# Delta-rule triangular systems of a diffusion block: layout change through DRAM instead of VectorE transposes, forward systems solved in transposed form

## The chip, the cores and the metric

The kernel runs on one core of a Trainium2 chip. The metric is device time in microseconds (us) of one execution on that core, the median of several runs. A profile of one execution goes with it: its instructions per engine (PE, the matmul engine; DVE, VectorE; ACT, ScalarE; POOL, GpSimd; SP, which issues most DMAs), their waits, and the granted clock of the matmul engine.

## The reference

One block over 512 latent tokens with 256 context tokens, width 1024, all in fp32: three token mixers in parallel (a chunked gated DeltaNet with 8 heads in both directions, a Hyena long convolution, an RG-LRU), each projected and merged by gates computed from the input, then a gated convolutional FFN. The change lies in the DeltaNet. Per head, direction and 64-token chunk it needs the inverse of a unit triangular 64x64 matrix:

```
m = jnp.where(strict, jnp.einsum('bhnid,bhnjd->bhnij', kb, k) * decay, 0.0)
eye = jnp.eye(cs, dtype=m.dtype)
t_inv = lax.linalg.triangular_solve(eye + m, ..., left_side=True, lower=True)
u = jnp.einsum('bhnij,bhnjd->bhnid', t_inv, v * beta[..., None])
w = jnp.einsum('bhnij,bhnjd->bhnid', t_inv, kb * jnp.exp(gc)[..., None])
```

A scan over the 12 chunks follows, forward and backward, and uses `t_inv` in each step.

## The kernel before, in words

**Weights and projections.** Every projection takes a weight tile of 128x1024 in fp32. `load_w` (L164) loads it by a DMA on SP's queue (L168) into one of three raw buffers; `split` makes a high part (L155 on ACT, L157 on POOL) and a low part, raw minus high (L160, on POOL or DVE), each in a ring of two; PE then runs three matmuls per product (L173 to L175, `mm3`). A raw buffer is free for the next DMA once its low part has been made, so SP's L168 waits for L160. A gate tile (24 projections of 512 columns, evicted by ACT at L594, stored by SP at L595) and a value tile (24 of 512 and 24 of 256 columns, evicted by ACT L502 and DVE L505 to L507, then ACT L903, six PE transposes L911, ACT L912, store L913) alternate in the part around the change. Names in this text: v0 to v7 are the value tiles, g0 to g11 the gate tiles.

**The systems.** `gram` (L803) multiplies keys by keys on PE and masks the products on DVE into three SBUF tiles: `M1[0]` and `M1[1]` hold the chunks that each direction needs first, `M3` the rest of both. Each 64x64 matrix is split in two 32x32 diagonal blocks and an off-diagonal one. `solve` (L831) handles one tile: it brings its 128 diagonal blocks into a layout of one block per partition, by 4 DVE transposes of 32 partitions x 1024 (L839), sets X to the identity on POOL (L841, L842), runs 31 elimination steps of a multiplication (L847) and a subtraction (L849) on DVE, brings the inverses back by 4 transposes (L857) and makes a transposed copy of two quarters by 2 more (L859, `Wu`). The off-diagonal blocks follow: per eighth, 16 matmuls for z (L873), a copy on ACT (L874), 16 matmuls for r (L877), a copy on ACT (L878). The finished matrices go to the DRAM tile `wad` by SP (L886, L893), from which the scan steps load them.

**What sets the order.** A scheduler orders the instructions of every engine when the kernel is built, and each engine and each DMA queue works through its list strictly in order. `run` (L931) offers it the pieces: `solve_first(0)` and `solve_first(1)` with v0, g0 to v5, g5, then `solve_second` (tile `M3`) with v6, g6, v7, g7 and g8 to g11. After that come the 12 scan steps (`step`, L996; their matmuls at L1025, L1035, L1043), which alternate with half gate tiles and with pieces of the modulation (L1068 to L1074). The first instruction that needs the second solve's result on PE is the z block L873 of `M3`, and the first one behind its r blocks in the changed kernel is the scan's L1043.

Of the kernel before, what the change touches and what calls it, by code (L numbers as in the profile page):

```python
# [10 lines left out]
F32 = mybir.dt.float32  # L11
F32R = mybir.dt.float32r
AF = mybir.ActivationFunctionType
ALU = mybir.AluOpType
# [3 lines left out]
P = 128  # L18
# [43 lines left out]
def seq(off, kb, n):  # L62
    return [off + kb * i for i in range(n)]
# [10 lines left out]
def tile_block(ctx: ExitStack, tc: tile.TileContext, I: dict, out: bass.AP, dbg=None, upto=99):  # L74
    nc = tc.nc
    sb = ctx.enter_context(tc.tile_pool(name="sb", bufs=1))
    pp = ctx.enter_context(tc.tile_pool(name="pp", bufs=1, space=PSUM))
    dr = ctx.enter_context(tc.tile_pool(name="dr", bufs=1, space=DRAM))
# [4 lines left out]
    def shaped(ap, shape):  # L83
        shape = list(shape)
        if len(shape) == 2:
            return ap
        names = "abcde"[:len(shape) - 1]
        return ap.rearrange("p (%s) -> p %s" % (" ".join(names), " ".join(names)),
                            **{n: d for n, d in zip(names[1:], shape[2:])})

    def at(off, shape, dt=F32, kb=None):

        n = int(np.prod(shape[1:]))
        size = int(kb * 256) if kb else n
        assert n <= size and off * 256 + size <= ARENA * 256, (shape, off, kb)
        key = (off, size, dt)
        if key not in regions:
            regions[key] = nc.alloc_sbuf_tensor_at(f"region{len(regions)}", [P, size], dt, offset=base + int(off * 1024)).ap()
        return shaped(regions[key][0:shape[0], 0:n], shape)

    def ring(kb, offs):
        return Ring(at, kb, offs)
# [22 lines left out]
    act = nc.scalar.activation  # L125
    stt = nc.vector.scalar_tensor_tensor
    vtt = nc.vector.tensor_tensor
    gtt = nc.gpsimd.tensor_tensor
    mmul = nc.tensor.matmul
    load = nc.sync.dma_start  # L130
# [627 lines left out]
    M1 = [at(84 + 8 * d, [P, 4, NH, 64]) for d in range(2)]  # L758
    M3 = at(100, [P, 2, 2, NH, 64])
    first, second = {0: [0, 1, 2, 3], 1: [0, 1, 4, 5]}, {0: [4, 5], 1: [2, 3]}  # L760
# [39 lines left out]
                act(KQ[h // 4][:, h % 4, :, 0, :], tp.rearrange("p n (c i) -> p (n c) i", i=64), AF.Copy)  # L800


    def gram(i, hf):  # L803
        lat, hs = i >= 2, slice(hf * 4, hf * 4 + 4)
        gp = dn([P, 4, 2, 64] if lat else [P, 4, 64])
        for h in range(4):
            for c in range(2):
                rc = slice(c * 64, c * 64 + 64)
                if lat:
                    kq = KQ[hf][:, h, (i - 2) * 2 + c]  # L810
                    mmul(gp[rc, h], kq[:, 0, :], kq, start=True, stop=True)
                else:
                    kt = KTc[hf][:, h, (i * 2 + c) * 64:(i * 2 + c + 1) * 64]
                    mmul(gp[rc, h, :], kt, kt, start=True, stop=True)
        g_ = gp[:, :, 0, :] if lat else gp
        for d in range(2):
            db = DB[d][i][:, hs, :]
            if i in first[d]:
                vtt(M1[d][:, first[d].index(i), hs, :], g_, db, op=ALU.mult)
            else:  # L820
                for c in range(2):
                    rc = slice(c * 64, c * 64 + 64)
                    vtt(M3[d * 64:d * 64 + 64, second[d].index(i), c, hs, :], g_[rc], db[rc], op=ALU.mult)
            if lat:
                at_ = atr([P, 4, 64])
                vtt(at_, gp[:, :, 1, :], db, op=ALU.mult)
                load(wad[d, i, :, 1, hf * 256:hf * 256 + 256], at_.rearrange("p h i -> p (h i)"))

    vtr = nc.vector.transpose

    def solve(dirs, M, NX_, tmr, eng):  # L831


        N, X = NX_
        tt_ = vtt if eng == "dve" else gtt
        for qd in range(4):
            b, d = qd % 2, dirs[qd // 2]
            rows_ = slice(qd * 32, qd * 32 + 32)
            vtr(N[rows_] if d == 0 else N[rows_].rearrange("p j i -> p i j"),  # L839
                M[rows_, :, b * 32:b * 32 + 32].rearrange("p a i -> p i a"))  # L840
        nc.gpsimd.memset(X, 0.0)  # L841
        nc.gpsimd.memset(X.rearrange("p a b -> p (a b)")[:, ::33], 1.0)  # L842
        yield
        for j in range(31):
            r = 31 - j
            tmp = tmr([P, r, j + 1])
            tt_(tmp, N[:, j + 1:, j].unsqueeze(2).to_broadcast([P, r, j + 1]),  # L847
                X[:, j, 0:j + 1].unsqueeze(1).to_broadcast([P, r, j + 1]), op=ALU.mult)
            tt_(X[:, j + 1:, 0:j + 1], X[:, j + 1:, 0:j + 1], tmp, op=ALU.subtract)  # L849
            yield  # L850

        Wu = N
        for qd in range(4):
            b, d = qd % 2, dirs[qd // 2]
            rows_ = slice(qd * 32, qd * 32 + 32)
            xi = X[rows_] if d == 0 else X[rows_].rearrange("p j i -> p i j")
            vtr(M[rows_, :, b * 32:b * 32 + 32].rearrange("p a i -> p i a"), xi)  # L857
            if b == d:
                vtr(Wu[rows_].rearrange("p a j -> p j a"), xi.rearrange("p i j -> p j i"))  # L859
        yield  # L860

        Z = X.rearrange("p a b -> p (a b)")
        for half in range(2):
            zp = dn([P, 16, 32])
            rp = dn([P, 16, 32])
            for c in range(2):
                d = dirs[c]
                pj = slice(c * 64 + d * 32, c * 64 + d * 32 + 32)
                pi = slice(c * 64 + (1 - d) * 32, c * 64 + (1 - d) * 32 + 32)
                ci = slice((1 - d) * 32, (1 - d) * 32 + 32)  # L870
                for a in range(16):
                    e = half * 16 + a
                    mmul(zp[pi, a, :], M[pj, e, ci], Wu[pj, e, :], start=True, stop=True)  # L873
                act(Z[pi, half * 512:half * 512 + 512], zp[pi].rearrange("p a b -> p (a b)"), AF.Copy)  # L874
                for a in range(16):
                    e = half * 16 + a
                    mmul(rp[pj, a, :], Z[pi, e * 32:e * 32 + 32], M[pi, e, ci], start=True, stop=True)  # L877
                act(M[pj, half * 16:half * 16 + 16, ci], rp[pj], AF.Copy, scale=-1.0)  # L878
            yield

    def solve_first(d):
        yield from solve((d, d), M1[d].rearrange("p t h i -> p (t h) i"),
                         [at(158 + 14 * d + 4 * i, [P, 32, 32]) for i in range(2)], ring(1, seq(166 + 2 * d, 1, 2)),
                         "dve")
        for a, i in enumerate(first[d]):
            load(wad[d, i, :, 0, :], M1[d][:, a].rearrange("p h i -> p (h i)"))  # L886

    def solve_second():
        yield from solve((0, 1), M3.rearrange("p t c h i -> p (t c h) i"),
                         [at(180 + 4 * i, [P, 32, 32]) for i in range(2)], ring(1, seq(188, 1, 2)), "dve")  # L890
        for d in range(2):
            for t, i in enumerate(second[d]):
                load(wad[d, i, :, 0, :].rearrange("(c j) x -> j c x", c=2),  # L893
                     M3[d * 64:d * 64 + 64, t].rearrange("p c h i -> p c (h i)"))
# [21 lines left out]
    for h in range(NH + 2):  # L916
        if h < NH:
            kss_[h] = key(h)
        if h == 0:
            query_out(NH - 1, sqs[NH - 1])  # L920
        if 0 < h <= NH:
            kns_[h - 1] = key_out(h - 1, kss_[h - 1])
        if h > 1:
            key_cols(h - 2, kns_[h - 2])
        if h >= 6:
            for i in [(0, 1), (2,), (3, 4), (5,)][h - 6]:
                gram(i, 0)
    for i in (0, 1, 4, 5, 2, 3):
        gram(i, 1)
# [26 lines left out]
    gates = [lambda f=f: gate(*f, "act", "pool") for f in fill[:NFILL]]  # L956
    work = [w_ for p_ in zip(values, gates) for w_ in p_] + values[len(gates):] + gates[len(values):]
    run([solve_first(0), solve_first(1)], work[:NW1])
    run([solve_second()], work[NW1:])
    for nm, x_ in (("kdd", kdd), ("vd", vd), ("rowd", rowd)):  # L960
        dump(nm, x_)
# [667 lines left out]
```

## Time and profile before

| | us |
|---|---|
| runs | 2179.06, 1700.55, 1703.49 |
| median | 1703.49 |
| the profiled execution: its own time | 1699.04 |
| the profiled execution: span, first to last instruction | 1696.9 |
| mean granted clock of TensorE in it | 0.957 of full |

The first run was disturbed and is far above the other two. The median is a measured time of the whole program; the span leaves out 2.1 us around the first and last instruction. The trace gives times from the start of the span; the part with the systems lies between 560 and 780 us.

### The profile page before, as it was taken

To read this page: it belongs to the slowest core of one execution; us is meant where nothing else is said; L and a number is where in the kernel's file an instruction comes from. 1 tells how busy PE (TensorE), PEld (TensorE's weight loads), DVE (VectorE), ACT (ScalarE), POOL (GpSimd) and SP (SyncE) were. 2 spreads that over 40 slices of the span, in tenths; PEclk is the share of its full clock that TensorE was granted. 3 is DMA by queue.
4 is the path that set the end of the run, shared out by engine and by line. 5 is a ranking of instruction groups with operands and counts; after the bars stand their busy time and mean duration, and the time that the engine had idled before them with its cause. 6 is when DMAs were issued, how large, how long until landed. Compare 5 with 4: busy or idle time off the path is not lost. (4 is left out here: it accounts for less than half of the span.)

```text
span 1696.9 us, 23679 instructions
## 1 busy us (share of the span) xinstructions
PE 1554.4 (92%) x9176; PEld 1264.1 (74%) x9176; DVE 1202.8 (71%) x1756; ACT 618.8 (36%) x1014; POOL 587.0 (35%) x407
## 2 busy tenths in 40 slices
PE   6989989889999988987899999999999999999998
PEld 1657767668787766875687777778878788888876
DVE  4677798765655999553675566777665899989873
ACT  3447878753454222231111150332222433333311
POOL 3752444433535351221333313222321234333441
PEclk7989999989999998788999999999999999999999
DMA  8522222234534332467889646322452123232331
GB/s 304 183 93 69 81 74 70 98 111 136 166 108 135 117 92 90 124 196 190 243 238 247 220 173 229 112 87 86 157 191 89 63 87 99 95 104 93 106 112 50
DMA packets 93057, 225.66 MB, mean 133 GB/s; under 512 B 9963, under 2 KB 30699, under 8 KB 92176
## 3 DMA queue, kind: packets, MB, share of 16 engines
q1 hardware_dynamic: 92112, 217.86, 40.9%
q0 software_dynamic: 832, 6.29, 0.9%
q8 instruction: 72, 1.18, 0.3%
q14 instruction: 41, 0.34, 0.1%
HBM read 190.45 MB, written 33.66 MB: 132 GB/s over the span
## 5 line engine op out<-in xcount | busy, mean ns | idle before, releaser
L173 PE MATMUL bank<-region,region 128*128 128x512 f32 (+1 forms) x2032 | 761.4, 376 | 23.8 <-DVE region L507 7.6
L175 PE MATMUL bank<-region,region 128*128 128x512 f32 (+1 forms) x2032 | 755.4, 373 | 24.6 <-DVE region L160 21.3
L174 PE MATMUL bank<-region,region 128*128 128x512 f32 (+1 forms) x2032 | 756.9, 373 | 5.0 <-DVE region L439 2.9
L173 PEld LDWEIGHTS bank<-region,region 128*128 128x128 f32 x2032 | 389.5, 192 | 101.6 <-ACT region L539 9.0
L175 PEld LDWEIGHTS bank<-region,region 128*128 128x128 f32 x2032 | 389.7, 192 | 97.7 <-DVE region L160 27.8
L174 PEld LDWEIGHTS bank<-region,region 128*128 128x128 f32 x2032 | 390.3, 192 | 69.6 <-DVE region L439 4.9
L160 DVE TENSOR_TENSOR region<-region,region 128x1024 fp32r<-128x1024 f32 (+2 forms) x241 | 269.8, 1133 | 173.0 <-ACT region L155 94.9
L155 ACT ACTIVATE region<-region 128x1024 fp32r<-128x1024 f32 (+2 forms) x209 | 178.4, 865 | 427.4 <-PE bank L174 130.0
L160 POOL TENSOR_TENSOR region<-region,region 128x1024 fp32r<-128x1024 f32 (+1 forms) x64 | 155.3, 2431 | 251.2 <-ACT region L155 210.8
L157 POOL TENSOR_SCALAR region<-region 128x1024 fp32r<-128x1024 f32 (+1 forms) x96 | 113.0, 1178 | 337.8 <-PE bank L174 151.2
L1443 DVE SCALAR_TENSOR_TENSOR region<-bank,pc,region 128x441 f32<-128x441 f32 (+2 forms) x352 | 224.8, 688 | 4.3 <-ACT region L1432 0.7
L505 DVE SCALAR_TENSOR_TENSOR region<-bank,pc,region 128x511 f32<-128x511 f32 (+1 forms) x56 | 34.1, 630 | 51.1 <-ACT region L502 47.3
L1074 DVE SCALAR_TENSOR_TENSOR region<-region,cc,region 128x1024 f32<-128x1024 f32 x28 | 42.1, 1504 | 35.9 <-DMA region<-in_w_mod_dram 35.5
L1012 POOL TENSOR_TENSOR region<-region,region 128x512 f32<-128x512 f32 x32 | 45.8, 1460 | 38.3 <-DMA region<-rowd 37.3
L502 ACT ACTIVATE region<-bank,pc 128x512 f32<-128x512 f32 (+1 forms) x40 | 23.0, 597 | 96.2 <-PE bank L175 96.2
L1455 POOL TENSOR_TENSOR region<-region,region 128x512 f32<-128x512 f32 x22 | 34.3, 1560 | 66.1 <-DVE region L1443 52.2
L1048 DVE SCALAR_TENSOR_TENSOR region<-region,egl,bank 128x128 f32<-128x128 f32 x160 | 42.3, 340 | 19.2 <-PE bank L1043 19.2
L1025 PE MATMUL bank<-region,region 128*64 128x128 f32 x608 | 38.9, 287 | 9.4 <-DVE region L1048 9.3
L1025 PEld LDWEIGHTS bank<-region,region 128*64 128x64 f32 x608 | 35.9, 145 | 14.6 <-DVE region L1048 6.3
L1037 ACT ACTIVATE region<-bank 128x512 f32<-128x512 f32 x24 | 14.3, 598 | 88.1 <-PE bank L1035 87.7
L594 ACT ACTIVATE region<-bank 128x512 f32<-128x512 f32 x32 | 18.8, 587 | 70.1 <-PE bank L175 66.0
L1035 PE MATMUL bank<-region,region 64*64 64x128 f32 x384 | 28.3, 298 | 12.7 <-DVE region L1029 6.9
(286 smaller groups left out, 1697.1 us busy)
## 6 DMA issues: line engine op xcount, KB each, us to landing
region<-in_w_in_dram SPq DMA_DIRECT2D x97, 512.0 KB, 3.6
region<-in_w_mod_dram SPq DMA_DIRECT2D x48, 512.0 KB, 6.7
region<-in_ffn_up_dram SPq DMA_DIRECT2D x44, 512.0 KB, 3.5
region<-in_w_proj_dram SPq DMA_DIRECT2D x24, 512.0 KB, 3.7
region<-in_ffn_down_dram SPq DMA_DIRECT2D x22, 512.0 KB, 3.4
gated<-region SPq DMA_DIRECT2D x32, 256.0 KB, 2.1
region<-gated SPq DMA_DIRECT2D x32, 256.0 KB, 3.5
kdd<-region SPq DMA_DIRECT2D x16, 384.0 KB, 2.8
```

The source lines that it names most:

```text
L155: act(hi, raw, AF.Copy)
L157: nc.gpsimd.tensor_scalar(hi, raw, 1.0, 0.0, op0=ALU.mult, op1=ALU.add)
L160: (vtt if e_lo == "dve" else gtt)(lo, raw, hi.bitcast(F32), op=ALU.subtract)
L173: mmul(ps, lh, rh, start=start, stop=False)
L174: mmul(ps, lh, rl, start=False, stop=False)
L175: mmul(ps, ll, rh, start=False, stop=stop)
L1012: gtt(wq[d][:, hs], KQ[hf][:, :, chs[d] - 4], eg[:, hs].unsqueeze(2).to_broadcast([P, 4, 2, 64]), op=ALU.mult)
L1025: mmul(X[hf][rcs[d], h, :], wq[d][:, hf * 4 + h, kind], S[d][:, hf * 4 + h, :], start=(kind == 0 or h == 0), stop=(kind == 0))
L1048: stt(S[d][:, h], S[d][:, h], egl[:, d, c, i, h:h + 1], p3[hf][d][:, h % 4], op0=ALU.mult, op1=ALU.add)
L1074: stt(acc, w_, cc[:, k, 0:1], acc, op0=ALU.mult, op1=ALU.add)
L1443: stt(uv[:, ro, co], pv_[:, ri, ci], w[:, a * 3 + b:a * 3 + b + 1], uv[:, ro, co], op0=ALU.mult, op1=ALU.add)
L1455: gtt(uu[0], uu[0], uu[1], op=ALU.mult)
```

## The change

Two DRAM tiles are added, `md` for the masked matrices and `xd` for the inverses. `gram` stores each tile of `M1` and `M3` to `md` as soon as its second half is masked (12 stores). `solve` loads its blocks from `md` straight into the one-per-partition layout, by 4 loads of 32x32 pieces of 32 fp32 numbers. Forward systems are needed transposed there: in `solve_first(0)` the elimination runs on the transposed form instead (`upper`: same operations, same sizes, with the index order reversed), and in `solve_second` the forward half is loaded into X and copied transposed into N by ACT. After the elimination ACT makes a transposed copy of X in N (L867), both are stored to `xd` (L868, L869), and 4 loads bring the inverses into M (L872) and 2 the transposed ones into `Wu` (L874). In all 30 DVE transposes go; 48 DMAs (12 + 12 + 6 + 18) on SP's queue and 4 ACT copies come. In the changed kernel z is L888, r L892, their copies L889 and L893, the stores of finished matrices L900 and L907, the elimination L861 and L863, the scan's matmuls L1039, L1049 and L1057, the value transposes L925.

```diff
     def gram(i, hf):
...
             if i in first[d]:
-                vtt(M1[d][:, first[d].index(i), hs, :], g_, db, op=ALU.mult)
+                t = first[d].index(i)
+                vtt(M1[d][:, t, hs, :], g_, db, op=ALU.mult)
+                if hf:
+                    load(md[d, :, t * 8:t * 8 + 8, :], M1[d][:, t])
...
+                if hf:
+                    t = second[d].index(i)
+                    load(md[2, d * 64:d * 64 + 64, t * 16:t * 16 + 16, :], M3[d * 64:d * 64 + 64, t].rearrange("p c h i -> p (c h) i"))
...
-            vtr(N[rows_] if d == 0 else N[rows_].rearrange("p j i -> p i j"),
-                M[rows_, :, b * 32:b * 32 + 32].rearrange("p a i -> p i a"))
+            load((N if upper or d else X)[rows_], md[n, rows_, :, b * 32:b * 32 + 32].rearrange("j a i -> a j i"))
+        if not upper and 0 in dirs:
+            act(N[0:64], X[0:64].rearrange("p j i -> p i j"), AF.Copy)
...
+            if upper:
+                to, row = slice(0, r), slice(r, 32)
+                of = r
+            else:
+                to, row = slice(j + 1, 32), slice(0, j + 1)
+                of = j
...
         Wu = N
...
-            vtr(M[rows_, :, b * 32:b * 32 + 32].rearrange("p a i -> p i a"), xi)
+        act(N, X.rearrange("p j i -> p i j"), AF.Copy)
+        load(xd[n, 0], X)
+        load(xd[n, 1], N)
+        for b, d, rows_ in quads:
+            there = int(not (upper or d))
+            load(M[rows_, :, b * 32:b * 32 + 32], xd[n, there, rows_].rearrange("a j i -> j a i"))
             if b == d:
-                vtr(Wu[rows_].rearrange("p a j -> p j a"), xi.rearrange("p i j -> p j i"))
+                load(Wu[rows_], xd[n, 1 - there, rows_].rearrange("a i j -> i a j"))
```

The scheduler then builds another order. Three places of it follow.

SP, before: what the queue holds where the finished first matrices are stored (L886), with weight loads (L168) between; no load that a solve needs stands there.

```order
L886 DMA wad<-region_2966 128x512 x2
L595 DMA gated<-region_4108 128x512
L168 DMA region_720<-in_w_in_dram 128x1024
L886 DMA wad<-region_2966 128x512 x2
L886 DMA wad<-region_2967 128x512 x2
```

SP, after: the same stores (now L900; region_2966 is `M1[0]`, region_2967 `M1[1]`), with the loads of the second `Wu` quarter (L874) and the last load into the second solve's N (region_4895, L846).

```order
L168 DMA region_902<-in_w_in_dram 128x1024
L874 DMA region_3880<-xd 32x32x32
L872 DMA region_2967<-xd 32x32x32 x2
L874 DMA region_3880<-xd 32x32x32
L927 DMA vd<-region_3099 128x6x128
L900 DMA wad<-region_2966 128x512 x4
L900 DMA wad<-region_2967 128x512 x2
L595 DMA gated<-region_4122 128x512
L846 DMA region_4895<-md 32x32x32
L900 DMA wad<-region_2967 128x512 x2
```

The last input of the second solve has moved behind six stores of finished first matrices and one gate store.

DVE, before: the second solve's start (region_4875 is its N, region_4876 its X), behind the transposes of the first two.

```order
L859 STREAM_TRANSPOSE region_3866<-region_3867 32x32x32
L857 STREAM_TRANSPOSE region_2967<-region_3867 32x32x32 x2
L859 STREAM_TRANSPOSE region_3866<-region_3867 32x32x32
L847 TENSOR_TENSOR region_4883<-region_4875,region_4876 128x31
L849 TENSOR_TENSOR region_4876<-region_4876,region_4883 128x31
```

DVE, after: the second solve's start (region_4895 is its N, region_4896 its X).

```order
L505 SCALAR_TENSOR_TENSOR region_3088<-bank_64,pc,region_3088 128x511
L506 SCALAR_TENSOR_TENSOR region_3088<-bank_64,pc,region_3088 128x511
L507 SCALAR_TENSOR_TENSOR region_3088<-bank_64,pc,region_3088 128x510
L160 TENSOR_TENSOR region_722<-region_902,region_721 128x1024
L861 TENSOR_TENSOR region_4904<-region_4895,region_4896 128x31
L863 TENSOR_TENSOR region_4896<-region_4896,region_4904 128x31
```

The second solve has moved behind the evictions of v7 and one low part of a weight tile, that of the gate tile g12 which the scan's first half gate uses.

PE, before: the second solve's z and r (region_2968 is `M3`), behind g11 and ahead of the scan's L1035.

```order
L175 MATMUL bank_66<-region_80,region_442 128x512
L873 MATMUL bank_67<-region_4875,region_2968 32x32 x16
L873 MATMUL bank_69<-region_4875,region_2968 32x32 x16
...
L873 MATMUL bank_69<-region_4875,region_2968 32x32 x16
L877 MATMUL bank_70<-region_2968,region_4876 32x32 x16
L1035 MATMUL bank_65<-region_5420,region_147 64x128 x8
L1035 MATMUL bank_66<-region_5420,region_147 64x128 x8
```

PE, after: the last z and r blocks of the second first-solve (region_2967), behind the last projection of g10.

```order
L175 MATMUL bank_65<-region_80,region_722 128x512
L888 MATMUL bank_67<-region_2967,region_3881 32x32 x16
...
L892 MATMUL bank_68<-region_2967,region_3881 32x32 x16
L925 MATMUL bank_67<-ident,region_3022 128x128 x2
L925 MATMUL bank_68<-ident,region_3022 128x128 x4
L173 MATMUL bank_66<-region_80,region_441 128x512
```

PE, after: the second solve's z and r (region_4895 is `Wu`), some 48 rows further on.

```order
L1049 MATMUL bank_66<-region_5444,region_147 64x128 x8
L173 MATMUL bank_63<-region_80,region_721 128x512
...
L175 MATMUL bank_63<-region_80,region_722 128x512
L888 MATMUL bank_67<-region_4895,region_2968 32x32 x16
L888 MATMUL bank_69<-region_4895,region_2968 32x32 x16
...
L892 MATMUL bank_70<-region_2968,region_4896 32x32 x16
L1057 MATMUL bank_69<-region_1199,region_5445 128x128
```

Six blocks of z and r of the first systems have come between g10 and g11, g11 has come behind them, and the second solve's blocks stand behind the scan's first L1049 and 12 projections, directly ahead of L1057.

## Rows read from the trace of the kernel before

**Rows 1.** The page, part 1: busy time, share and instructions of PE.
```profile
PE 1554.4 (92%) x9176; PEld 1264.1 (74%) x9176; DVE 1202.8 (71%) x1756; ACT 618.8 (36%) x1014; POOL 587.0 (35%) x407
```

**Rows 2.** Busy by stretch: length, PE, PEld, DVE, ACT, POOL, clock, DMA share, GB/s.
```profile
600.00:620.00 20.00, 15.45 (x68) 12.93 (x69) 20.00 (x56) 5.87 (x9) 13.90 (x2) 0.83 0.24 75
...
680.00:700.00 20.00, 20.00 (x196) 16.83 (x195) 5.02 (x13) 3.53 (x6) 1.42 (x2) 0.50 0.24 80
...
760.00:780.00 20.00, 13.65 (x134) 11.50 (x132) 4.34 (x4) 4.49 (x9) 0.00 (x0) 0.62 0.68 179
```

**Rows 3.** Groups by line, 545 to 800 us: busy, mean ns, idle before, releaser.
```profile
L160 POOL TENSOR_TENSOR region<-region,region 128x1024 fp32r<-128x1024 f32 x18 | 57.8, 3216 | 89.8 <-ACT region L155 89.8
...
L839 DVE STREAM_TRANSPOSE region<-region 32x1024 f32<-32x1024 f32 x12 | 25.4, 2120 | 0.3
L857 DVE STREAM_TRANSPOSE region<-region 32x1024 f32<-32x1024 f32 x12 | 25.3, 2104 | 0.3
...
L155 ACT ACTIVATE region<-region 128x1024 fp32r<-128x1024 f32 x18 | 19.0, 1056 | 19.6 <-PE bank L174 12.4 <-DMA wad<-region 3.2 <-issue 2.5
...
L859 DVE STREAM_TRANSPOSE region<-region 32x1024 f32<-32x1024 f32 x6 | 11.9, 1990 | 0.0
...
L1074 DVE SCALAR_TENSOR_TENSOR region<-region,cc,region 128x1024 f32<-128x1024 f32 x7 | 9.0, 1285 | 21.3 <-DMA region<-in_w_mod_dram 21.2
...
L874 ACT ACTIVATE region<-bank 32x512 f32<-32x512 f32 x12 | 7.1, 588 | 18.5 <-PE bank L873 15.3 <-DVE region L857 3.2
```

**Rows 4.** PE's timeline: start, length, line, shape, count, idle before and releaser.
```profile
571.95 0.82 PE L911 MATMUL bank<-ident,region 128*128 128x128 f32 x6
...
601.26 0.58 PE L173 MATMUL bank<-region,region 128*128 128x256 f32 x1 [4.17 <-DVE region L507]
...
615.16 0.79 PE L175 MATMUL bank<-region,region 128*128 128x512 f32 x1 [3.29 <-POOL region L160]
...
630.11 0.82 PE L911 MATMUL bank<-ident,region 128*128 128x128 f32 x6
...
644.61 0.82 PE L911 MATMUL bank<-ident,region 128*128 128x128 f32 x6
...
650.83 1.91 PE L873 MATMUL bank<-region,region 32*32 32x32 f32 x32 [5.41 <-DVE region L859]
...
660.11 1.19 PE L873 MATMUL bank<-region,region 32*32 32x32 f32 x32 [0.94 <-DVE region L859]
...
777.40 1.83 PE L1043 MATMUL bank<-region,region 64*128 64x128 f32 x28
```

**Rows 5.** DVE's timeline in the second solve: start, length, line, shape, count.
```profile
674.67 0.21 DVE L847 TENSOR_TENSOR region<-region,region 128x31 f32<-128x31 f32 x1
...
685.00 0.42 DVE L847 TENSOR_TENSOR region<-region,region 128x255 f32<-128x255 f32 x1
...
717.60 2.40 DVE L849 TENSOR_TENSOR region<-region,region 128x156 f32<-128x156 f32 x1
...
736.43 2.09 DVE L859 STREAM_TRANSPOSE region<-region 32x1024 f32<-32x1024 f32 x1
```

**Rows 6.** POOL's timeline: start, length, line, shape, count, idle before.
```profile
603.56 13.90 POOL L160 TENSOR_TENSOR region<-region,region 128x1024 fp32r<-128x1024 f32 x2 [9.10 <-ACT region L155]
...
632.04 2.40 POOL L160 TENSOR_TENSOR region<-region,region 128x1024 fp32r<-128x1024 f32 x1 [1.32 <-ACT region L155]
```

**Rows 7.** DMA issues: names, queue, count, KB each, median us to landing.
```profile
gated<-region SPq DMA_DIRECT2D x32, 256.0 KB, 2.1
...
kdd<-region SPq DMA_DIRECT2D x16, 384.0 KB, 2.8
region<-kdd SPq DMA_DIRECT2D x24, 256.0 KB, 7.6
```

**Rows 8.** Line L827 (stores to `wad`), SP's queue: issue time in ns, min/median/max.
```profile
L827 SPq DMA_DIRECT2D wad<-region x16: 319/320/655, 543.0 to 584.0; - x16
```

More of the change, by code (lines that the diff above doesn't have):

```diff
@@ L800, in key_cols @@
                 act(KQ[h // 4][:, h % 4, :, 0, :], tp.rearrange("p n (c i) -> p (n c) i", i=64), AF.Copy)
+    md, xd = dr.tile([3, P, 32, 64], F32, name="md"), dr.tile([3, 2, P, 32, 32], F32, name="xd")
     def gram(i, hf):
@@ L827, in gram, with solve @@
                 load(wad[d, i, :, 1, hf * 256:hf * 256 + 256], at_.rearrange("p h i -> p (h i)"))
-    vtr = nc.vector.transpose
-    def solve(dirs, M, NX_, tmr, eng):
+    def solve(n, dirs, M, NX_, tmr):
         N, X = NX_
[L835 to L838, printed above, removed]
-            vtr(N[rows_] if d == 0 else N[rows_].rearrange("p j i -> p i j"),
-                M[rows_, :, b * 32:b * 32 + 32].rearrange("p a i -> p i a"))
+        upper = dirs == (0, 0)
+        quads = [(qd % 2, dirs[qd // 2], slice(qd * 32, qd * 32 + 32)) for qd in range(4)]
+        for b, d, rows_ in quads:
+            load((N if upper or d else X)[rows_], md[n, rows_, :, b * 32:b * 32 + 32].rearrange("j a i -> a j i"))
+        if not upper and 0 in dirs:
+            act(N[0:64], X[0:64].rearrange("p j i -> p i j"), AF.Copy)
         nc.gpsimd.memset(X, 0.0)
@@ L845, in solve @@
             r = 31 - j
+            if upper:
[4 more added lines that the diff above has]
+                of = j
             tmp = tmr([P, r, j + 1])
-            tt_(tmp, N[:, j + 1:, j].unsqueeze(2).to_broadcast([P, r, j + 1]),
-                X[:, j, 0:j + 1].unsqueeze(1).to_broadcast([P, r, j + 1]), op=ALU.mult)
-            tt_(X[:, j + 1:, 0:j + 1], X[:, j + 1:, 0:j + 1], tmp, op=ALU.subtract)
+            vtt(tmp, N[:, to, of].unsqueeze(2).to_broadcast([P, r, j + 1]),
+                X[:, of, row].unsqueeze(1).to_broadcast([P, r, j + 1]), op=ALU.mult)
+            vtt(X[:, to, row], X[:, to, row], tmp, op=ALU.subtract)
             yield
         Wu = N
[L853 to L856, printed above, removed]
-            vtr(M[rows_, :, b * 32:b * 32 + 32].rearrange("p a i -> p i a"), xi)
+        act(N, X.rearrange("p j i -> p i j"), AF.Copy)
+        load(xd[n, 0], X)
+        load(xd[n, 1], N)
+        for b, d, rows_ in quads:
+            there = int(not (upper or d))
+            load(M[rows_, :, b * 32:b * 32 + 32], xd[n, there, rows_].rearrange("a j i -> j a i"))
             if b == d:
-                vtr(Wu[rows_].rearrange("p a j -> p j a"), xi.rearrange("p i j -> p j i"))
+                load(Wu[rows_], xd[n, 1 - there, rows_].rearrange("a i j -> i a j"))
         yield
@@ L881, in solve_first @@
     def solve_first(d):
-        yield from solve((d, d), M1[d].rearrange("p t h i -> p (t h) i"),
-                         [at(158 + 14 * d + 4 * i, [P, 32, 32]) for i in range(2)], ring(1, seq(166 + 2 * d, 1, 2)),
-                         "dve")
+        yield from solve(d, (d, d), M1[d].rearrange("p t h i -> p (t h) i"),
+                         [at(158 + 14 * d + 4 * i, [P, 32, 32]) for i in range(2)], ring(1, seq(166 + 2 * d, 1, 2)))
         for a, i in enumerate(first[d]):
@@ L888, in solve_second @@
     def solve_second():
-        yield from solve((0, 1), M3.rearrange("p t c h i -> p (t c h) i"),
-                         [at(180 + 4 * i, [P, 32, 32]) for i in range(2)], ring(1, seq(188, 1, 2)), "dve")
+        yield from solve(2, (0, 1), M3.rearrange("p t c h i -> p (t c h) i"),
+                         [at(180 + 4 * i, [P, 32, 32]) for i in range(2)], ring(1, seq(188, 1, 2)))
         for d in range(2):
```

## The prediction

> **What bounds the kernel now.** I read the busy shares first: PE is busy 92% of the span, so only idle or slowly clocked PE time is there to gain [rows 1]. Then the stretches of 20 us around the systems: while DVE runs the two interleaved first solves at 20.00 of 20, PE falls to 15.45; later PE is busy throughout at a granted clock of 0.50 (the 1.2 GHz level), and before the scan it is busy 13.65 of 20 at 0.62 [rows 2]. Then the groups by line: DVE spends 25.4 + 25.3 + 11.9 = 62.6 us on the transposes that the change removes [rows 3]. Last PE's timeline, which tells what of that PE feels: waits of 4.17 for an eviction queued behind solve steps on DVE, of 3.29 for a low part on POOL, of 5.41 for the transposes out. Blocks of 32x32 matmuls take 1.19 us each at full clock and 1.91 at half [rows 4].
>
> The event that I follow is L1043 of the first scan step (L1057 after), at 777.40 [rows 4]. All the changed work stands ahead of it, the rest of the program is alike, and PE is what ends last there. How much could be had? One pair of gate and value tile with its transposes took 644.61 - 630.11 = 14.50 us without a wait. It holds 60 units of 512 columns (48, and 24 halves), so a unit is 0.242 us, transposes included. From the transposes at 571.95 to L1057 PE has, by the new order, 492 such units, 24 blocks of z and r, and L1049: 119 + 29 + 2 = 150 us, which would end at 722. So 55 us are lost now, and the question is how many come back.
>
> **The change part by part, as a sum.**
>
> *DVE.* It loses 62.6 us, but PE's path gets only what it waited for. It pays with DMAs and with a new order, and the latter costs most.
>
> *Until the first z.* The new order puts it behind four pairs, g5, v6 and 10 matmuls of g6: 571.95 + 4 x 14.50 + (24 + 36 + 10) x 0.242 = 646.9. No eviction is late any more, since the transposes in are gone. One wait stays: the low part of v5 falls into the interleaved solves, where POOL took 13.90 us for two such operations, against 2.40 for one outside [rows 6]. I add 13.90 / 2 - 2.40 = 4.5, giving 651.4. Below this it can be 0, above it 11.5 (all of the excess on one).
> By the Trainium skill ("SBUF — State Buffer", section "SBUF: two separate sides") DVE and GpSimd share a port pair as an exclusive lock held for one instruction. The trace agrees that one holds the other up, but several instructions long; were it only one DVE step the term would be near zero, and the forecast about 4 us less.
>
> *Loads and stores.* The 12 N loads and 18 loads back each have 1024 pieces of 128 bytes (128 KB); no such load is in the trace. From below I take the 256 KB store of 2.1 us, from above the load of `kdd`, 7.6. The store of `kdd`, 768 pieces in 384 KB, is nearest in the number of pieces: 2.8 [rows 7]. I take 3.1 (2.8 scaled between the two stores by pieces; an estimate). The 12 `md` stores and N loads of the first solves lie beside v3 to v5 on PE and cost nothing there; without that cover they would cost two landings, 6 us. An issue takes 0.32 to 0.66 us of SP [rows 8]; 48 of them are some 20 us, spread over 200 us in which SP mostly waits.
>
> *First z to the end of g10.* By the order 146 units and 10 blocks: 146 x 0.242 + 10 x 1.19 = 47.2. I add one wait of 3.5, the size of those in [rows 4]: ACT's new copy L867 of `M1[1]` waits for that solve and stands ahead of v7's evictions (between 0 and 8, the latter two such waits). g10 ends at 651.4 + 50.7 = 702.1.
>
> *The second solve.* This is the step that decides. Its DVE steps began at 674.67 [rows 5]. In the new order its last N load (L846, region_4895) stands on SP behind the stores L900 of finished matrices of `M1[1]`, and these need the z, copy, r, copy behind g10: 1.19 + 0.59 + 1.19 + 0.59 = 3.6 (copies by L874, 588 ns [rows 3]). Four issues at some 0.45 make 1.8, the landing 3.1. The solve starts at 702.1 + 8.5 = 710.6. (The low part of g12, ahead of it on DVE, needs only the end of g10 and about 2.3 us, so is hidden behind the load.) Alone it takes 21.5: 674.67 to 685.42 is 10.75 for half of its 62 instructions, whose sizes mirror [rows 5]. One low part on POOL holds a step up for 2.40, and three pieces of the modulation at 1.285 each now stand in between [rows 3, 5]: it ends at 710.6 + 21.5 + 2.4 + 3.9 = 738.4. Before, its transposes ended at 736.43 + 2.09 = 738.5.
>
> *Out of the second solve.* ACT's copy 1.05 (by L155, 128x1024, contiguous; the strided read may cost double), store 2.8, `Wu` load 3.1, issues 1.5: 8.5, so z starts at 746.9. Nothing covers this; queued behind on PE are z, r and all of the scan. PE has been idle before and is at half clock, as in the same place before: 8 x 1.91, and about 2 for copies not covered, end at 764.2.
>
> *Sum.* 777.40 - 764.2 = 13.2 earlier. The 12 projections that come ahead of this and L1057 itself run at the 1.2 GHz level, which gives back 12 x 0.23 = 2.8. Net 10.4: 1699.0 - 10.4 = 1688.6, so **1689 us** against the profiled execution's 1699.04. The median of the runs shown is 1703.49, which is 0.3% above that execution; I leave that offset out of the point and give it to the range.
>
> **The rivals.**
>
> *R1, PE is the bound and data comes in time.* No wait on POOL or ACT, landings of 2.1, no modulation piece between, full clock: g10 ends at 694.1, the solve starts at 701.1, ends at 722.6, its data is back at 729.1, and 8 x 1.19 + 2 ends at 740.6: 36.8 earlier, **1662**. For it: waits named in [rows 4] come from DVE work that goes. Against it: the N load's place on SP is fixed, whatever DVE saves.
>
> *R2, the small pieces are expensive.* Three landings lie on the path (first `Wu`, the second solve's N, its `Wu`). Each T us over 3.1 costs 3T. At 7.6, as for `kdd` loads, 3 x 4.5 = 13.5: 1702, no gain. Slower by over 2% from T = 15, a landing of 18 us. Against it: 768 pieces landed in 2.8.
> The Trainium skill ("DMA: Bandwidth & Descriptors", section "Rules for kernel authors") says that a plain DMA with a rearranged access pattern is 19 times slower than the hardware transpose. Applied to the 2.8 us it would be about 53 us a load and about 1840 us in all (an estimate). Only blocks of 128 bytes are reordered here, and no load of the trace shows such a price, so I hold it unlikely.
>
> *R3, in-order queues give the gain back.* SP holds loads that solves need behind weight loads L168, which wait for low parts on POOL, and ACT holds evictions behind copies that wait for DVE or a landing. If the excess of one held POOL operation, 13.90 - 2.40 = 11.5 us, goes onto the path at both the first `Wu` load and the second solve's start, that is +23: **1712**. It decides from 10.4 us on: above that the kernel is slower than before. For it: PE already waited 3.29 for POOL during the solves, and six more loads now queue behind L168. Against it: the weight ring's low parts must be done anyway before PE needs them.
>
> *R4, the change doesn't do what it says:* the DVE time goes, but PE ends where it did: 1699; it is part of R3's band.
>
> **How the numbers follow.** Forecast (1675 to 1700) 0.58, R1 (1645 to 1672) 0.14, R3 with R4 (1700 to 1733) 0.21, R2 and R3 beyond that (above 1733) 0.07. A measurement of this kernel tells about 2%, 34 us, from no change. Faster by more takes most of R1 and a little of the forecast: 0.15. Slower by more takes R2 and R3's end: 0.09. The rest, 0.76, is within 2%. The range 1660 to 1715 leaves out half of R1 below, and R2 and a third of R3 above; it holds the `kdd` bound of the landings (1702) and both ends of the POOL term.
>
> **What would show it.** No transposes on DVE in the solves. First z near 651 and g10's end near 702. Loads of 32x32 pieces at about 3 us. The second solve's first L861 near 711, waiting for the load of region_4895, about 36 us later than L847 began. PE idle for 10 us or more ahead of the last z blocks, at half clock behind it, and L1057 near 764. I am wrong if those loads land in over 8 us, if the second solve starts before 700, if PE is not idle ahead of its z, or if a wait of the scan behind L1057 takes the gain.

## The result, and the profile after

The changed kernel takes 1723.66 us (median of 4 runs, 1719.06 to 1729.45) against 1703.03 before (now with a fourth run): ratio 1.0122, 95% interval 1.0084 to 1.0159. It is slower by 1.2%, outside the range on record (1660 to 1715) and on the other side of the forecast. Its profiled execution has a span of 1719.7 us, 22.8 more than before.

The page's part 1 after (for [rows 1]):

```profile
PE 1563.0 (91%) x9176; PEld 1271.7 (74%) x9176; DVE 1142.3 (66%) x1726; ACT 628.4 (37%) x1018; POOL 573.8 (33%) x407
```

DVE lost 60.5 us, about the 62.6 of the transposes [rows 3]; the instruction count of PE is the same, and it is 8.6 us longer busy.

The sum on record ended at the scan's first L1057. PE's timeline after, at the events it was made of (for [rows 4]; start, length, line, shape, count, idle before and releaser):

```profile
624.23 0.50 PE L175 MATMUL bank<-region,region 128*128 128x512 f32 x1 [1.80 <-POOL region L160]
...
653.89 1.19 PE L888 MATMUL bank<-region,region 32*32 32x32 f32 x32
...
702.07 1.19 PE L888 MATMUL bank<-region,region 32*32 32x32 f32 x32
...
751.07 3.43 PE L888 MATMUL bank<-region,region 32*32 32x32 f32 x61 [11.59 <-DMA region<-xd]
...
764.27 4.02 PE L1057 MATMUL bank<-region,region 64*128 64x128 f32 x32
...
778.14 0.69 PE L1039 MATMUL bank<-region,region 128*64 128x128 f32 x2 [6.87 <-POOL region L1028]
```

The second solve on DVE after, its first and its last multiplication (for [rows 5]):

```profile
710.34 0.21 DVE L861 TENSOR_TENSOR region<-region,region 128x31 f32<-128x31 f32 x1 [5.96 <-DMA region<-md]
...
738.86 0.18 DVE L861 TENSOR_TENSOR region<-region,region 128x31 f32<-128x31 f32 x1
```

First z at 653.89 (forecast 651.4), end of g10, where the next z begins, at 702.07 (702.1), second solve from 710.34 (710.6) to 739.3 (738.4), its z at 751.07 (746.9), L1057 at 764.27 (764.2). Up to there the change gained 777.40 - 764.27 = 13.1 us, as forecast. The last row shows what comes next: PE waits 6.87 us for POOL at the first matmuls of step 1.

The stretch of the scan from the first to the last of the 11 steps' L1043 (before) and L1057 (after), one row each (columns as in [rows 2]):

```profile
777.40:948.90 171.50, 152.25 (x1655) 127.00 (x1654) 102.46 (x207) 24.77 (x42) 54.63 (x43) 0.97 0.84 226
```

```profile
764.30:971.10 206.80, 171.00 (x1655) 143.12 (x1654) 105.53 (x210) 26.07 (x44) 60.16 (x50) 0.86 0.77 212
```

The same 1655 records of PE take 35.3 us longer. PE's idle time in them is 35.80 instead of 19.25, 16.6 more; its busy time 171.00 instead of 152.25, 18.8 more, at a mean granted clock of 0.86 instead of 0.97. So here the waiting came with about as much again in slower work; the ratio is no constant (18.0 us more busy time beside 37.0 more idle in the run all_prio below). 13.1 - 35.3 = -22.2 is the whole difference of the spans but 0.6.

What PE waits for in the scan after (waits: line, releaser, us in total, times, longest):

```profile
PE bank L1039 <- POOL region L1026: 21.4, 11, 6.9
PE bank L1039 <- POOL region L1028: 10.8, 4, 6.9
```

Before, the scan has no such row; its largest is a state update on DVE:

```profile
PE bank L1025 <- DVE region L1048: 9.3, 4, 5.9
```

L1026 and L1028 are POOL's products of queries or keys with a step's decay row (`rowd`), and POOL in turn waits for the load of that row (L1007 before, L1021 after). SP's queue shows where these loads stand. Its timeline around step 7's decay rows, before (start, length, line, names, count):

```profile
871.01 0.33 SPq L595 DMA_DIRECT2D gated<-region  x1
871.44 1.49 SPq L1007 DMA_DIRECT2D region<-rowd  x2
873.02 8.04 SPq L1070 DMA_DIRECT2D region<-in_w_mod_dram  x4
```

and after:

```profile
880.26 0.38 SPq L595 DMA_DIRECT2D gated<-region  x1
880.73 0.38 SPq L1084 DMA_DIRECT2D region<-in_w_mod_dram  x1
881.16 0.51 SPq L1007 DMA_DIRECT2D region<-kdd  x1
881.72 0.60 SPq L1005 DMA_DIRECT2D region<-vd  x1
882.36 0.59 SPq L1006 DMA_DIRECT2D region<-wad  x1
883.00 0.60 SPq L1007 DMA_DIRECT2D region<-kdd  x1
883.70 1.01 SPq L1021 DMA_DIRECT2D region<-rowd  x2
```

The rows stood right behind the gate store; now a modulation load and four chunk loads are ahead of them, with the store 1.8 MB in 3.4 us, which at the 212 GB/s of the scan is over 8 us of transfer (an estimate). POOL's product began 4.4 us after the issue before, and 9.3 us after it in the changed kernel, one row each:

```profile
875.86 5.96 POOL L1012 TENSOR_TENSOR region<-region,region 128x512 f32<-128x512 f32 x4 [4.60 <-DMA region<-rowd]
...
893.01 6.92 POOL L1026 TENSOR_TENSOR region<-region,region 128x512 f32<-128x512 f32 x4 [7.92 <-DMA region<-rowd]
```

From the issue of a step's first row to PE's first use of its product, the median over the 11 steps fell from 18.0 us to 10.8 (from the timelines of SP and PE).

DMA issues, the median us to landing in the last column: the decay rows before (first row) and after, and (for [rows 7]) the new transfers:

```profile
region<-rowd SPq DMA_DIRECT2D x22, 256.0 KB, 4.7
...
region<-rowd SPq DMA_DIRECT2D x22, 256.0 KB, 7.5
...
md<-region SPq DMA_DIRECT2D x12, 256.0 KB, 3.5
...
xd<-region SPq DMA_DIRECT2D x6, 512.0 KB, 7.6
...
region<-xd SPq DMA_DIRECT2D x18, 128.0 KB, 4.0
...
region<-md SPq DMA_DIRECT2D x12, 128.0 KB, 4.1
```

The 7.6 of the stores to `xd` is the one landing that the trace has of the six, that of the store issued at 664.7.

### The profile page after: what moved, and what is told of

It reads as the page before. It is cut to its first block, busy times and chain, and to the rows that moved or that the text cites. A ratio compares the mean times of both kernels' runs of the same rounds, so it can differ in the third digit from the quotient of the medians.

```text
span 1719.7 us, 23708 instructions
## 1 busy us (share of the span) xinstructions
PE 1563.0 (91%) x9176; PEld 1271.7 (74%) x9176; DVE 1142.3 (66%) x1726; ACT 628.4 (37%) x1018; POOL 573.8 (33%) x407
## 5 line engine op out<-in xcount | busy, mean ns | idle before, releaser
L160 POOL TENSOR_TENSOR region<-region,region 128x1024 fp32r<-128x1024 f32 (+1 forms) x64 | 142.5, 2230 | 253.2 <-ACT region L155 204.0
L1039 PE MATMUL bank<-region,region 128*64 128x128 f32 x608 | 57.5, 353 | 34.4 <-POOL region L1026 21.4
L1039 PEld LDWEIGHTS bank<-region,region 128*64 128x64 f32 x608 | 50.7, 185 | 42.9 <-POOL region L1026 28.2
L1026 POOL TENSOR_TENSOR region<-region,region 128x512 f32<-128x512 f32 x32 | 45.4, 1451 | 36.3 <-DMA region<-rowd 36.3
L502 ACT ACTIVATE region<-bank,pc 128x512 f32<-128x512 f32 (+1 forms) x40 | 23.3, 597 | 77.4 <-PE bank L175 76.4
L861 DVE TENSOR_TENSOR region<-region,region 128x31 f32<-128x31 f32 (+15 forms) x93 | 35.5, 391 | 8.1 <-DMA region<-md 6.0
```

The source lines that it names most:

```text
L160: (vtt if e_lo == "dve" else gtt)(lo, raw, hi.bitcast(F32), op=ALU.subtract)
L861: vtt(tmp, N[:, to, of].unsqueeze(2).to_broadcast([P, r, j + 1]), X[:, of, row].unsqueeze(1).to_broadcast([P, r, j + 1]), op=ALU.mult)
L1026: gtt(wq[d][:, hs], KQ[hf][:, :, chs[d] - 4], eg[:, hs].unsqueeze(2).to_broadcast([P, 4, 2, 64]), op=ALU.mult)
L1039: mmul(X[hf][rcs[d], h, :], wq[d][:, hf * 4 + h, kind], S[d][:, hf * 4 + h, :], start=(kind == 0 or h == 0), stop=(kind == 0))
```

## The experiments

Theory A: the loss is the place of the decay-row loads on SP. Rivals: B, the new DMAs make loads slow wherever they stand; C, the scan is bound by its bytes; D, the new solve order itself. Times are medians; ratios are to the kernel before, run on the same chip. "Scan" is the stretch of the two rows above: 171.5 us before, 206.8 after; the pitch of the expectations is a tenth of it. Scans and waits come from one profiled execution of each kernel. Most lie within 3 us of the median; in_only's is 7.7 us above it, and those of before, before_eg_late, before_rowd_first and rowd_pool are 4.0, 4.3, 7.7 and 11.3 below.

**rowd_prio.** The decay-row loads raised in priority.

```diff
-            load(eg, rowd[1, d, chs[d]].partition_broadcast(P))
+            with tc.high_priority():
+                load(eg, rowd[1, d, chs[d]].partition_broadcast(P))
```

> The changed kernel with one edit: the scan's decay-row loads (rowd) get a higher priority, so that five of them stand on SP ahead of the last N load and the gate stores, as before the change. Theory A (the scan lost its lookahead: PE waits 32 us for POOL's products, because the rowd loads stand behind a gate store and the chunk loads): PE's wait for POOL falls below 8 us, the scan's pitch from L1057 to L1057 falls from 20.7 to about 17.5, the time to 1685-1700. Theory B (the order is not the cause; the small pieces and more bytes load the DMA queues and the rowd loads land late wherever they stand): pitch stays above 19.5, time 1710-1725. The second solve may start up to 8 us later, since a rowd load that waits for POOL now stands ahead of or near its N load.

Measured 1743.76, ratio 1.0237 (1.0220 to 1.0254), scan 215.6. PE's wait for POOL is gone and the rows land in 3.8 us, against B; but the time is worse than either theory's range. SP's longest wait in it (from 690 us on):

```profile
SPq L1022 <- POOL region L1027: 62.9, 12, 14.7
```

A row's load must wait until POOL has released its buffer; put too early it stands at the head of the queue, and SP stood waiting for 62.9 us. PE waits for DVE instead (its largest wait in the scan is 15.5 us, for a state update). So the test did not settle A: it traded one queue for the other.

**in_only, out_only.** One half of the change each; the other half as before.

```diff
 in_only
-        act(N, X.rearrange("p j i -> p i j"), AF.Copy)
-        load(xd[n, 0], X)
...
+            nc.vector.transpose(M[rows_, :, b * 32:b * 32 + 32].rearrange("p a i -> p i a"), xi)
 out_only
-        upper = dirs == (0, 0)
+        upper = False
...
+            nc.vector.transpose(N[rows_] if d == 0 else N[rows_].rearrange("p j i -> p i j"),
```

> Only the way in goes through DRAM (12 stores, 12 loads, transposed form of the forward first solve); the way out is 18 DVE transposes, as before. The order puts the first z back behind v4 and the second solve's z and r ahead of the scan's first L1046 (= L1049). If the way out through DRAM is what turns the change into a loss: 1675-1698. If any trip through DRAM costs more than the transposes: 1703 or above. Scan pitch 17-18.5 in the first case.

> Only the way out goes through DRAM (6 stores, 18 loads, 3 copies on ACT); the way in is 12 DVE transposes, as before. If the way out is what loses: 1710-1730, with a scan pitch above 19.5 since the first rowd loads stand as late as in the changed kernel. If the loss is made by the loads in (last N load behind the stores of finished matrices): 1695-1705.

in_only: 1690.66, ratio 0.9937 (0.9914 to 0.9960). out_only: 1735.81, ratio 1.0187 (1.0166 to 1.0208). The halves add up: -12.5 and +32.6 are +20.1, near the change's +20.6, which may be chance, since each half gets an order of its own. out_only lies 6 us above its range. In in_only's profile the way in brings L1057's counterpart to 759.4, 18 us earlier, and then loses most of it: scan 186.2, with

```profile
PE bank L1036 <- POOL region L1023: 21.1, 11, 4.9
```

out_only starts its scan at 782.1, 4.7 later than before, and needs 205.0 for it, with 31.7 us of PE waiting for POOL. So each half alone, the way in too, brings the waits for the decay rows' products.

**all_prio.** As rowd_prio, with the N loads, the `xd` stores and the loads back in high priority too.

> The changed kernel with a higher priority on its own N loads, on the stores and loads of the inverses, and on the scan's rowd loads. The order puts the first systems' z and r close together, the second solve's ahead of the first L1049. Theory A: PE's wait for POOL in the scan below 8 us, the last N load no longer behind the stores of finished matrices, so second solve earlier than 705, L1057 at 740-760, time 1665-1690. Theory B: above 1700.

Measured 1757.63, ratio 1.0325 (1.0307 to 1.0343), scan 226.5, with 57.4 us of SP waiting for POOL at these loads. The time is B's (above 1700), the mark of A is there too (PE's wait for POOL is gone), and the rest of A fails: L1057 comes at 782.9. As in rowd_prio, SP's wait explains it and neither theory.

**rowd_pool, in_rowd_pool.** The decay-row loads on POOL's queue, in the changed kernel and in in_only.

```diff
-            load(eg, rowd[1, d, chs[d]].partition_broadcast(P))
+            nc.gpsimd.dma_start(eg, rowd[1, d, chs[d]].partition_broadcast(P))
```

> The changed kernel with the scan's 22 decay-row loads issued by POOL's queue instead of SP's; the products that use them stand on POOL too, so they wait for no other engine's queue, and SP neither holds them back nor is held by them. Theory A (the loss in the scan is the place of these loads on SP, behind gate stores and chunk loads): scan pitch 17-18, time 1685-1700, PE's wait for POOL below 10 us. Theory C (the scan is bound by the bytes that it must load, some 50 MB, and can't end earlier): PE's waits move to the chunk loads, pitch stays at 20 or more, time 1715-1725.

> The way in through DRAM, the way out by DVE transposes, and the decay-row loads on POOL's queue. Its scan began 18 us earlier than before the change with the way in alone, and lost all 18 again with 21 us of PE waiting for POOL. Theory A: most of the 18 stays, 1670-1682. Theory C: 1688-1697, as without this edit.

rowd_pool: 1710.10, ratio 1.0044 (1.0015 to 1.0074), scan 181.1: 13.6 us of the loss are back, a time between the two theories' ranges. in_rowd_pool: 1698.84, ratio 0.9983 (0.9961 to 1.0005), scan 187.0, not better than in_only and just above C's range. More of POOL's own work then falls into the scan (its busy time there is 74 us, 54 in in_only), and PE waits for DVE instead (26.1 us). Half for A, half against.

**after_half_mod, before_half_mod.** Half of the modulation pieces left out.

```diff
-        for k in range(4) if s_ % 3 < 2 else ():
+        for k in range(2) if s_ % 3 < 2 else ():
```

> The changed kernel with half of the modulation pieces left out (16 loads of 512 KB and 16 DVE operations fewer, all within the scan; the modulation sums are incomplete). Theory C (bytes): 8.4 MB at some 0.22 MB per us give 30 us or more back, 1685-1695. Theory A (place of the decay-row loads behind gate stores and chunk loads): the backlog ahead of them is shorter, at most half of it comes back, 1705-1718.

> The kernel before the change with the same half of the modulation pieces left out. Theory C: the scan before is as bound by bytes as the one after, so it gains about as much, 30 us: 1670-1675. Theory A: PE hardly waits for loads in it, so it gains less than 12: 1691-1703.

After: 1696.41, ratio 0.9965 (0.9946 to 0.9984), 27 us less than the changed kernel; scan 174.4, PE's wait for POOL 4.1. Before: 1697.24, ratio 0.9973 (0.9953 to 0.9992), only 6 less; scan 171.7, as with all pieces. The second run speaks against C: the scan before isn't bound by bytes. The first lies outside A's range and 1.4 above C's. In it the decay rows land in 5.7 us, so with fewer bytes ahead of them the bad place seems to cost little; but the edit also takes 16 DVE operations away, and this pair doesn't tell the two apart.

**before_eg_late.** In the kernel before, the decay rows can't be loaded ahead of the second solve's end.

```diff
-    egr = ring(2, seq(176, 2, 2))
-    rvr = ring(2, seq(180, 2, 3) + [194])
+    egr = ring(2, [182, 184])
+    rvr = ring(2, [176, 178, 180, 194])
```

> The kernel before the change with two SBUF buffers exchanged: the scan's decay rows take addresses in the second solve's buffers, so that none of these loads can be issued ahead of the second solve's end (before: five of them). Nothing of the change is in it. Theory A (the loss is the lost lookahead of the decay rows): PE waits for POOL in the scan appear, 15-35 us, pitch 19-21, time 1715-1735. Theory D (the loss has its cause in the new DMAs or the changed solve order itself): no such waits, 1698-1708.

Measured 1697.55, ratio 0.9966 (0.9941 to 0.9991), scan 167.0. No loss, though PE now waits 6.3 us for POOL and the rows land in 6.9 us, nearly the 7.5 of the changed kernel. So A in its first form falls: five rows loaded in advance are worth nothing here, and late landing alone does not make the loss either. Their issue still comes 12.7 us ahead of PE's use (median), against 10.8 in the changed kernel. D had no such waits and 1698 to 1708: its time nearly fits, its waits don't, and no run takes the new solve order alone.

**rowd_first, in_rowd_first, before_rowd_first, out_rowd_first.** In each step the decay-row loads are written ahead of the chunk loads.

```diff
-        v, kd, wa = chunk_loads(s, lat)
         wq = [None] * 2
         for d in range(2) if s else ():
...
+        v, kd, wa = chunk_loads(s, lat)
         rr, vt = [None] * 2, [None] * 2
```

> The changed kernel; in each scan step the decay-row loads are written ahead of the chunk loads instead of behind them, so that they stand ahead of them on SP, from step 1 on behind the first w_mod loads and not behind the first half gate's store. Theory A with the backlog as its cause (a decay row waits for some 1.8 MB issued just ahead of it): landing 4-5.5 us instead of 7.5, PE's wait for POOL below 15 us, pitch 18-19, time 1698-1710. If the place among the chunk loads doesn't matter and only the early five do: 1715-1725.

> The way in through DRAM, the way out by transposes, and the decay-row loads written ahead of the chunk loads. It had 21 us of PE waiting for POOL in the scan; with the backlog theory half or more of it goes: 1675-1686. Otherwise 1687-1698. If it beats both kernels by 1% it is the version to keep.

> The kernel before the change with the decay-row loads written ahead of the chunk loads, and nothing else. In it PE does not wait for POOL in the scan, so if the edit only mends what the change's order spoils: 1697-1706, and the 1674 of the way in with this edit is the way in's own gain. If the edit makes the scan faster in any kernel: 1675-1690.

> Only the way out through DRAM, with the decay-row loads ahead of the chunk loads. It was 33 us slower than before without this edit. If all of that was the place of these loads in the scan: 1698-1706. If the way out costs of itself (the inverses are fetched through DRAM ahead of z, the second solve starts later): 1710-1725, with the first scan block L1051 at 780 or later.

| kernel | us | ratio (95%) | without the edit | scan: without, with |
|---|---|---|---|---|
| rowd_first (whole change) | 1698.53 | 0.9973 (0.9944 to 1.0002) | 1723.66 | 206.8, 185.7 |
| in_rowd_first | 1674.05 | 0.9819 (0.9769 to 0.9870) | 1690.66 | 186.2, 161.9 |
| before_rowd_first | 1705.19 | 1.0017 (0.9990 to 1.0043) | 1703.03 | 171.5, 167.4 |
| out_rowd_first | 1719.19 | 1.0103 (1.0064 to 1.0142) | 1735.81 | 205.0, 185.6 |

The edit leaves the kernel before as it was and gives back 25 us to the changed one, 17 to each half. In rowd_first PE's waits for POOL at these matmuls are gone (32.2 us in the changed kernel); out_rowd_first keeps 5.7. So the place of these loads within a step is shown to be the loss's cause, for 25 us. The backlog ahead of them is not shown to be it: their median landing in rowd_first is still 7.1, not the 4 to 5.5 expected. They gain by being issued earlier, 16.6 us ahead of PE's use (median) instead of 10.8. The scan of rowd_first:

```profile
762.70:948.40 185.70, 161.82 (x1657) 134.92 (x1654) 100.68 (x209) 26.10 (x44) 55.21 (x45) 0.90 0.86 227
```

in_rowd_first is 1.8% faster than the kernel before and 2.9% faster than the changed one; its scan:

```profile
759.30:921.20 161.90, 151.61 (x1655) 126.53 (x1654) 93.06 (x205) 24.77 (x42) 53.66 (x45) 0.98 0.93 235
```

The way out stays a loss of its own, 14 us against before_rowd_first (1719.19 - 1705.19), 5.5 of it ahead of the scan (it starts at 780.6 instead of 775.1).

**n_rowd_first.** The whole change with the N loads in high priority and the decay rows first: the second solve no longer waits for the stores of finished matrices.

```diff
-            load((N if upper or d else X)[rows_], md[n, rows_, :, b * 32:b * 32 + 32].rearrange("j a i -> a j i"))
+            with tc.high_priority():
+                load((N if upper or d else X)[rows_], md[n, rows_, :, b * 32:b * 32 + 32].rearrange("j a i -> a j i"))
...
+        v, kd, wa = chunk_loads(s, lat)
         rr, vt = [None] * 2, [None] * 2
```

> The whole change with the N loads at a higher priority, so that the second solve's last load no longer stands behind the stores of the finished first matrices, and with the decay-row loads ahead of the chunk loads. The forecast held that this load sets the second solve's start (710): the solve then starts at 685-703, the last z comes 8-15 us earlier, 1683-1693. If something else starts it (the low part of g12 on DVE at 703), 1692-1700.

Measured 1719.06, ratio 1.0109 (1.0072 to 1.0146). The second solve ended at 682.2 instead of rowd_first's 738.5, 56 us earlier, and its z began at 745.2, only 4.3 earlier than there (749.5). The time was 20 us worse than rowd_first's and outside both ranges. The early result lay waiting: ACT had copied it by 684.2, but its stores to `xd` were issued at 731.45 and 734.79, behind stores of finished first matrices for which SP waited 21.0 us on ACT, and PE sat idle 7.02 us for the loads back, ahead of the same z. In this order the solve also interleaves with the first ones, whose first z slips from 654.5 to 664.0, and the scan starts at 772.7 instead of 762.7.

## Why the prediction was wrong

**The first part held, in part by luck.** Each event up to L1057 came within 5 us, and the gain of 13.1 us there is what the sum gave (13.2). The N load's place on SP did set the second solve's start: it was issued at 707.11, behind the stores that need the blocks begun at 702.07, and DVE waited 5.96 us for it.

```profile
707.11 0.46 SPq L846 DMA_DIRECT2D region<-md  x1
```

But terms of the sum were off and cancelled:

- Until the first z, the POOL term was 1.80 on PE, not 4.5, and "No eviction is late any more" was wrong by 2.92:

```profile
627.65 0.53 PE L173 MATMUL bank<-region,region 128*128 128x256 f32 x1 [2.92 <-DVE region L507]
```

- The term 4.5 came from a misreading. Of the two operations in the 13.90 us of [rows 6] one took 11.55 and the other 2.39, so the excess is 9.1, not 11.5. R3's two such terms are then +18 (1707), not +23.
- From the first z to the end of g10 the forecast wait of 3.5 didn't come: PE was busy for all 48.1 us.
- "10.75 for half of its 62 instructions" is the time of 29 of them; all 62 alone take about 23.3 by the same row, not 21.5. With the modulation pieces the solve took 28.9, where 27.8 was forecast.
- The way out of the second solve took 11.8 us (739.3 to 751.07) instead of 8.5: ACT's copy 1.99 instead of 1.05, the second store 4.4 until the loads behind it were issued instead of 2.8, the `Wu` load 3.6 instead of 3.1.

```profile
741.32 0.33 SPq L869 DMA_DIRECT2D xd<-region  x1
...
745.71 1.56 SPq L872 DMA_DIRECT2D region<-xd  x2
747.31 0.56 SPq L874 DMA_DIRECT2D region<-xd  x1
```

- The last eight blocks took 13.2 instead of 17.3: at the forecast half clock (0.50), but in 1.65 us a block instead of 1.91 and with no uncovered copy. "As in the same place before" is wrong for the second solve: its z of before, from 751.04, ran at 1.00.

The loads of small pieces landed in 4.0 and 4.1, between the bounds 2.1 and 7.6 and a microsecond above the value taken.

**The step that failed** is the sentence ahead of the sum: "All the changed work stands ahead of it, the rest of the program is alike". The sum put what comes behind L1057 at nothing. The instructions there are alike, their order on SP isn't: the decay-row loads had moved behind gate store, modulation and chunk loads, and the scan lost 35.3 us. The edit of rowd_first, which moves them forward, gives 21.1 of these back (206.8 to 185.7); the cause of the other 14.2 stays open. The text did name the last way to be wrong, "if a wait of the scan behind L1057 takes the gain", but gave it no price.

**A step left open** is "This is the step that decides", of the second solve. It was timed rightly. n_rowd_first, with the solve over 56 us earlier, brought PE to its z only 4 us sooner; but there the wait had moved to the stores on the way out, so what an early solve is worth with its way out free is not shown.

**The rivals.** R3, in-order queues give the gain back, comes nearest: 1712 forecast, 1723.66 measured, but its places were the weight loads and the `Wu` load, not the scan. Its mechanism, a queue in order that delays what a chain needs, is the one that the scan shows. R2 didn't happen: of the landings that the trace has, none is above 5.0. The rule of the Trainium skill weighed there ("DMA: Bandwidth & Descriptors", section "Rules for kernel authors"), 19 times for a rearranged access pattern, would have made some 53 us of a load (an estimate); the trace has 4.1 for pieces of 128 bytes. The SBUF port rule ("SBUF — State Buffer", section "SBUF: two separate sides") is not settled by this. Beside the steps of one lone solve the low part took 2.42 us, as outside, and a DVE step that began just after it took 2.50 where its neighbours take 0.42. Beside two interleaved solves two low parts took 6.47 together, the first 4.03:

```profile
608.51 2.42 POOL L160 TENSOR_TENSOR region<-region,region 128x1024 fp32r<-128x1024 f32 x1 [2.94 <-ACT region L155]
608.72 2.50 DVE L863 TENSOR_TENSOR region<-region,region 128x255 f32<-128x255 f32 x1
...
620.14 6.47 POOL L160 TENSOR_TENSOR region<-region,region 128x1024 fp32r<-128x1024 f32 x2 [9.21 <-DMA vd<-region]
```

**Open.** With the decay rows first, the scan still takes 185.7 and 185.6 us in the two kernels with the way out, and 161.9 and 167.4 in the two without. In the traces of the former PE waits for DVE, at state updates and modulation sums. Bytes are a rival that no run settles: by rate times length (an estimate) the scans with the way out move 42.2 and 42.5 MB at 227 and 229 GB/s, those without 38.0 and 38.5 MB at 235 and 230, and 4 MB at 230 GB/s are 17 us, about the difference. Part of it is modulation: with the way out 28 of its 48 loads of 512 KB are issued in the scan, in the other two 24. So C, which before_half_mod speaks against for the kernel before, is still open for what is left of the loss.

## What to carry to other kernels

Where a scheduler orders in-order queues, an edit in one stage can reorder the loads of the next: read the new order on to the end of the next stage, not to the end of the change, and compare for each load how long before its use it is issued. Here a load that feeds a chain (decay row, POOL product, matmul) did best ahead of the bulk loads of the same step; raised further it cost 20 us more, since its wait for a buffer then blocked the queue. Try the halves of a two-sided change apart: here the way in gains and the way out loses, and the way in with the scan's loads put in order is 1.8% faster than the kernel before.

## What the runs showed of the hardware

Loads of 1024 pieces of 128 bytes landed in 4.0 to 4.1 us (medians). A 512 KB store of the inverses landed in 7.6 in the one case that the trace has, and on the path the loads behind another could be issued 4.4 us after it. In the scan 16.6 us more of idle time on PE came with 18.8 us more of busy time for the same 1655 records, as the mean granted clock fell from 0.97 to 0.86.
